# A convolution's first banded weight tile on GpSimd, held behind a row of sums of squares

## The chip, the cores and the metric

The kernel runs on one core of one Trainium2 chip. The metric is the device time of one execution in microseconds (us), smaller is better; the time given for a kernel is the median of several executions.

The engines of the core work side by side, each through its own instructions in order: TensorE does matrix products (PE in the profile, and PEld for its weight loads), VectorE (DVE), ScalarE (ACT) and GpSimd (POOL) work on tiles of 128 partitions, and SyncE (SP) issues most of the DMAs. An engine waits for another only where an instruction waits on a semaphore.

## The reference

One step of a streaming encoder with two layers, width 1024, in float32. It treats 512 frames of a new stream (the prompt) and 8 running streams of 16 frames (the sample group). Only the first layer matters here, and of it the part up to the convolution:

```python
def conv_module(h, hist, g, w_pw1, b_pw1, w_dw, b_dw, ln_g, ln_b, w_pw2, b_pw2):
    a, gate = jnp.split(rms_norm(h, g) @ w_pw1 + b_pw1, 2, axis=-1)
    glu = a * jax.nn.sigmoid(gate)
    full = jnp.concatenate([hist.astype(glu.dtype), glu], axis=1)
    y = lax.conv_general_dilated(full, w_dw[:, None, :], ...) + b_dw
    y = jax.nn.silu(layer_norm(y, ln_g, ln_b))
    return h + y @ w_pw2 + b_pw2, full[:, -CONV_HIST:]
```

`rms_norm` divides each frame by the root of its mean square over the 1024 features. The convolution is depthwise (each feature by itself), 31 taps wide and causal. After it come a layer norm over the features, a product with a 1024x1024 matrix, and a gated feed-forward block; the second layer is attention and a second feed-forward block, and a last norm.

## The kernel before, in words

The activations `h` lie with features on the partitions: 8 chunks of 128 features, 640 frames along the free dimension. The frames are worked in two groups: group 0 is frames 0 to 255 (the 128 sample frames and the first 128 of the prompt), group 1, the larger one, is frames 256 to 639.

**Products.** Every float32 weight tile is split into a rounded high part and the rest (`wsplit`): ScalarE writes the high part (`whi`, L156), VectorE and GpSimd write the rest (`wlo`, L160), each a share. In the first products `pool=2`, so the second half of a tile's 2048 columns is GpSimd's. Activations are split likewise by `xsplit` (L165 ScalarE, L166 VectorE). A product is three matmuls (L176 to L178).

**Root mean square.** `rms` calls `rstd_bc`: eight squares of the chunks (`square`, L185 on ScalarE, L188 on VectorE or GpSimd) are added up one after the other by `colmean` into `acc` (L201), TensorE sums over the partitions (L210), VectorE adds epsilon (L232), GpSimd raises to the power -0.5 (L236), and TensorE spreads the result over 128 partitions (L222). Then VectorE forms the eight normed chunks `n` (L249), and `xsplit` makes the products' operand `x`. For group 0 the adds are on VectorE; for group 1 the adds and five of the squares are on GpSimd.

**Gated product and convolution.** `glu(c, g)` makes feature chunk c of the gated product; VectorE writes it into `gs` (group 0, L392) or `gp` (group 1, L401), and for group 0 four copies on GpSimd (L396 to L399) put the prompt's overlapping frames in place. Each chunk's convolution is done in one of three ways: on VectorE (`conv`, L440 and L443, written into PSUM), on ScalarE and GpSimd (`conv_pool`, L422 and L423), or on TensorE (`conv_pe`, L475). The last one needs what `conv_pe_load` prepares: the weight tile `w4`, 32 banded 32x32 blocks that one GpSimd multiply (L450) makes from `i4`, four identity blocks, and `dwv`, the taps that a DMA from ScalarE's queue brings (L373), and `x4`, four shifted copies of the chunk that go by DMA through memory (`sc`, L458, and `x<-sc`, L461). Both tiles have one buffer, so a second `conv_pe` waits for the first.

**What sets the order.** The string `PLAN` lists the steps in the order in which they are written: `a0 y a1 a2 a4 x a3 a5 a6 l04 p04 ...` means glu of chunks 0, 1, 2 and 4 for group 0, then `x`, the root mean square of group 1, then more glu, then `l04`, the load for the TensorE convolution of chunk 4 in group 0, and `p04`, that convolution. Within this a list scheduler places every instruction as early as its inputs allow, by a priority that the code can raise (`tc.high_priority`). `tc.issue_after(ins)` is an edge for the scheduler: what is written inside it is placed after `ins`.

The multiply for `l04` has inputs that are there from the beginning (`i4`, `dwv`), so it is placed near the head of GpSimd's row, ahead of everything that group 0 asks of GpSimd. The multiply's tile is first read by `p04`.

Of the kernel before, what the change touches and what calls it, by code (L numbers as in the profile page):

```python
# [11 lines left out]
ALU = mybir.AluOpType  # L12
PSUM = bass.MemoryType.PSUM

P = 128
# [60 lines left out]
V_DW, V_DW4, V_NDW = 0, KT * W, KT * W + KT * 32  # L76
# [3 lines left out]
def tile_trunk(ctx, tc, xT, vecs, hist, w_pw1, w_pw2, w_in0, w_out0, w_in1, w_out1,  # L80
               w_kq, w_v, w_o, rel, kc, vc, nfin, y_out, convp_out, convs_out, k_out, v_out):
    nc = tc.nc
# [13 lines left out]
    def nm(s):  # L96
        uid[0] += 1
        return f"{s}_{uid[0]}"
# [79 lines left out]
            nc.tensor.matmul(ps, wh, xl, start=False, stop=(i == last))  # L178

    last = {}  # L180

    def square(s, n, eng="a"):
        q = tp.tile([P, 384], F32, tag="sq", name=nm("sq"))
        if eng == "a":
            nc.scalar.activation(out=q[:, :n], in_=s, func=AF.Square)  # L185
        else:
            e = nc.vector if eng == "v" else nc.gpsimd
            e.tensor_tensor(out=q[:, :n], in0=s, in1=s, op=ALU.mult)  # L188
        return q[:, :n]
# [155 lines left out]
    dwv = cp.tile([P, V_NDW], F32, name="dwv", tag="dwv")  # L345
# [14 lines left out]
    i4 = cst.tile([P, 32 + XPAD], F32, name="i4", tag="i4")[:, 0:32]  # L360
# [86 lines left out]

    def conv_pe_load(c, g):
        w4 = cp.tile([P, 32, 32], F32, tag="w4", name=nm("w4"))
        nc.gpsimd.tensor_tensor(  # L450
            out=w4, in0=i4[:, None, :].to_broadcast([P, 32, 32]),
            in1=dwv[:, V_DW4 + 32 * c:V_DW4 + 32 * c + 32].unsqueeze(2).to_broadcast([P, 32, 32]),
            op=ALU.mult)
        full = GSW if g == 0 else GPW
        wd = full - 4
        src = gsf if g == 0 else gp
        sc = dr.tile([P, GSW], F32, tag="sc", name=nm("sc"))
        nc.sync.dma_start(sc[:, 0:full], src[:, c, :])  # L458
        x4 = cp.tile([P, 4, GSW], F32, tag="x4", name=nm("x4"))
        for s in range(4):  # L460
            nc.sync.dma_start(x4[32 * s:32 * s + 32, :, 0:wd],  # L461
                              sc[:, s:s + wd].rearrange("(q p) w -> p q w", q=4))
        return w4, x4
# [60 lines left out]
    def step(op, arg):  # L524
# [6 lines left out]
        elif op == "b":  # L531
            pw1(g, 1)
        elif op == "y":
            load_x(1)
        elif op == "x":
            xs[1] = rms(1, V_NCONV, SSQ1, 8)
        elif op == "l":
            x4s[g, cs[0]] = conv_pe_load(cs[0], g)
        elif op == "p":
            conv_pe(cs[0], g, *x4s[g, cs[0]])  # L540
        elif op == "q":
            conv_pool(cs[0], g)
        elif op == "d":
            conv(cs, g)
        elif op == "s":
            if g == 0:
                nc.sync.dma_start(convs_out, gs[:, :, 0:8, :])
            else:
                nc.sync.dma_start(convp_out, gp[:, :, 384:384 + HIST])
        elif op == "n":  # L550
            zs[g] = conv_ln(g)
        elif op == "w":
            pw2(g, zs[g])
        elif op == "r":
            late[g] = (R0, R1)[g](g, V_NFFN)
        elif op == "f":
            ffn({0: hp0}, w_in0, w_out0, {0: late[0]}, (0,), (chunks.pop(0),), PFA)
# [354 lines left out]
    xps = ExitStack()  # L912
    xp = xps.enter_context(tc.tile_pool(name="xp", bufs=1, **tr))

    def after(ins):
        return tc.issue_after(ins.ins) if ins is not None else ExitStack()

    def tmp(t):
        return tp.tile([P, 384], F32, tag=t, name=nm(t))[:, 0:HT]

# [35 lines left out]
    def plain(j, jj, q, wts):  # L956
        wh, wl = wts
        c = TH[q]
        ps = []
        for ab in range(2):  # L960
            pt = bank()
            o = [(8 * ab + (k + 4 * ab) % 8) * P for k in range(KT)]
            with after(marks.get((j, q, ab))):
                mm3(pt[:, :HT], [(wh[:, i:i + P], wl[:, i:i + P]) for i in o],
                    [(raw_slot[k // 4][q][0][:, k % 4, :], raw_slot[k // 4][q][1][:, k % 4, :])
                     for k in range(KT)])
            ps.append(pt[:, :HT])
        with tc.high_priority(offset=HP):
            gate(ps[0], ps[1], hids[0], jj, c)
# [230 lines left out]
    for j in range(NPL, FT):  # L1200
        c, jj = where[j]
# [112 lines left out]
```

## Time and profile before

| what | us |
|---|---|
| median of 3 executions | 1543.46 |
| lowest and highest of them | 1538.12, 1545.01 |
| the profiled execution, its own time | 1541.31 |
| span of its trace | 1539.5 |
| busy in the span: PE, DVE, ACT, POOL | 1467.9, 1049.0, 667.1, 447.3 |
| instructions on POOL | 406 |

The profile comes from a single execution, by the hardware profiler. A row of its timeline has the start in us from the span's beginning, the length in us, engine, line of the code, operation, what is written and read with its shape, how many instructions were merged, and in square brackets how long the engine had been idle before and what ended that wait. Rows overlap a little at their ends. In a table of stretches, PEclk is the share of full TensorE speed that was granted. "PE mm" rows are matmuls, "mm" being the tile in PSUM.

### The profile page before, as it was taken

How to read it: one execution, taken by the hardware profiler on the slowest of the kernel's cores; microseconds unless marked ns; L12 is line 12 of the kernel's file. 1: busy time of each engine (PE TensorE's matmuls, PEld its weight loads, DVE VectorE, ACT ScalarE, POOL GpSimd, SP SyncE). 2: the span in 40 equal slices, each digit the busy share in tenths (PEclk: the TensorE clock that was granted, in tenths of full speed). 3: DMA queues.
4: the chain of work that ended last, by engine and by line, in shares of the span. 5: the costliest groups of instructions: out<-in, count | busy, mean ns of one | idle time of the engine just before them, and what ended most of it. 6: DMA issues, size and time to landing. Idle time of an engine off the chain costs nothing.

```text
span 1539.5 us, 27212 instructions
## 1 busy us (share of the span) xinstructions
PE 1467.9 (95%) x11054; PEld 1397.9 (91%) x11054; DVE 1049.0 (68%) x1890; ACT 667.1 (43%) x1196; POOL 447.3 (29%) x406
## 2 busy tenths in 40 slices
PE   5988898989999999999999999999999999999998
PEld 5878878988999999999988798896989999999998
DVE  6994999989555444556577767666796467467456
ACT  4544455545423323235455445343564144244144
POOL 6965458987401000001322111110421011011010
PEclk9989899999999999999999999999999999999999
DMA  7884334454421333432555545444103222222222
GB/s 261 249 219 143 123 103 162 146 183 151 151 83 56 123 123 123 126 120 96 196 184 195 170 151 199 150 158 151 32 25 117 76 83 89 76 83 90 76 83 83
DMA packets 57022, 200.54 MB, mean 130 GB/s; under 512 B 10176, under 2 KB 20672, under 8 KB 44096
## 3 DMA queue, kind: packets, MB, share of 16 engines
q1 hardware_dynamic: 56608, 198.48, 39.1%
q8 instruction: 87, 1.43, 0.4%
q10 hardware_dynamic: 288, 0.31, 0.1%
q14 instruction: 39, 0.32, 0.1%
HBM read 187.55 MB, written 11.22 MB: 129 GB/s over the span
## 4 chain that ended last, share of the span: by engine, by line
PE 73%; DVE 15%; issue 3%; ACT 3%; POOL 3%; DMA 3%; SPq 0%; POOLq 0%; ACTq 0%; DVEq 0%
PE mm L176 13%; PE mm L177 13%; PE mm L178 13%; PE pb L977 6%; DVE w L443 4%; PE pc L977 4%; DVE wlo L160 4%; PE pa L977 3%; PE w L803 1%; PE pb L176 1%; PE pb L178 1%; PE pb L177 1%; PE pa L178 1%; PE pa L176 1%; PE pa L177 1%
## 5 line engine op out<-in xcount | busy, mean ns | idle before, releaser
L177 PE MATMUL mm<-x,wlo 128*128 128x256 f32 (+1 forms) x1344 | 417.8, 313 | 15.8 <-DVE wlo L160 15.4
L176 PE MATMUL mm<-x,whi 128*128 128x256 f32 (+1 forms) x1344 | 414.4, 312 | 9.2 <-ACT x L165 6.9
L178 PE MATMUL mm<-x,whi 128*128 128x256 f32 (+1 forms) x1344 | 413.0, 311 | 2.5 <-DVE x L166 2.5
L177 PEld LDWEIGHTS mm<-x,wlo 128*128 128x128 f32 x1344 | 257.1, 191 | 19.4 <-DVE wlo L160 18.3
L176 PEld LDWEIGHTS mm<-x,whi 128*128 128x128 f32 x1344 | 255.1, 191 | 14.1 <-ACT x L165 7.7
L178 PEld LDWEIGHTS mm<-x,whi 128*128 128x128 f32 x1344 | 255.3, 191 | 5.2 <-DVE x L166 4.1
L156 ACT ACTIVATE whi<-raw 128x2048 fp32r<-128x2048 f32 (+2 forms) x87 | 143.9, 1658 | 171.9 <-PE mm L178 105.1
L160 DVE TENSOR_TENSOR wlo<-raw,whi 128x2048 fp32r<-128x2048 f32 (+5 forms) x87 | 156.4, 1801 | 44.7 <-ACT whi L156 44.0
L922 POOL TENSOR_TENSOR raw<-raw 128x512 f32<-128x512 f32 x38 | 56.4, 1485 | 326.4 <-DVE raw L922 255.2
L177 PE MATMUL mm<-hid,wlo 128*128 128x256 f32 (+1 forms) x352 | 107.6, 308 | 6.1 <-DVE wlo L160 6.1
L160 POOL TENSOR_TENSOR wlo<-raw,whi 128x1536 fp32r<-128x1536 f32 (+3 forms) x33 | 93.0, 2822 | 55.1 <-ACT whi L156 55.1
L178 PE MATMUL mm<-hid,whi 128*128 128x256 f32 (+1 forms) x352 | 105.8, 307 | 0.8 <-DVE hid L166 0.7
L443 DVE SCALAR_TENSOR_TENSOR w<-gp,dwv,w 128x384 f32<-128x384 f32 x180 | 104.4, 613 | 0.9
L176 PE MATMUL mm<-hid,whi 128*128 128x256 f32 (+1 forms) x352 | 104.4, 307 | 0.0
L201 POOL TENSOR_TENSOR acc<-sq,sq 128x384 f32<-128x384 f32 (+1 forms) x8 | 8.1, 1006 | 255.8 <-ACT sq L185 255.8
L156 ACT ACTIVATE whi<-rx 128x2048 fp32r<-128x2048 f32 (+1 forms) x30 | 54.0, 1800 | 54.0 <-PE mm L178 42.0
L177 PEld LDWEIGHTS mm<-hid,wlo 128*128 128x128 f32 x352 | 66.0, 188 | 7.1 <-DVE wlo L160 7.1
L160 DVE TENSOR_TENSOR wlo<-rx,whi 128x2048 fp32r<-128x2048 f32 (+4 forms) x30 | 62.9, 2098 | 13.3 <-ACT whi L156 12.4
L423 POOL TENSOR_TENSOR y<-y,cvt 128x256 f32<-128x256 f32 (+1 forms) x60 | 67.9, 1132 | 4.3 <-ACT cvt L422 2.2
L178 PEld LDWEIGHTS mm<-hid,whi 128*128 128x128 f32 x352 | 65.7, 188 | 1.2 <-DVE hid L166 1.2
L176 PEld LDWEIGHTS mm<-hid,whi 128*128 128x128 f32 x352 | 65.1, 188 | 0.3 <-ACT hid L165 0.3
L165 ACT ACTIVATE whi<-raw 128x1024 fp32r<-128x1024 f32 x38 | 39.4, 1054 | 54.2 <-DVE raw L922 19.1
(329 smaller groups left out, 3648.2 us busy)
## 6 DMA issues: line engine op xcount, KB each, us to landing
raw<-in_w_in SPq DMA_DIRECT2D x49, 1024.0 KB
raw<-in_w_out SPq DMA_DIRECT2D x28, 768.0 KB
cache<-in_ck SPq DMA_DIRECT2D x32, 512.0 KB
cache<-in_cv SPq DMA_DIRECT2D x32, 512.0 KB
raw<-in_w_pw SPq DMA_DIRECT2D x14, 1024.0 KB
rx<-in_w_in SPq DMA_DIRECT2D x13, 1024.0 KB
rx<-in_w_pw SPq DMA_DIRECT2D x8, 1024.0 KB
raw<-in_w_kq SPq DMA_DIRECT2D x8, 1024.0 KB
```

The costliest lines, as they stand in the source:

```text
L156: nc.scalar.activation(out=hi[:, a:b], in_=raw[:, a:b], func=AF.Copy)
L160: eng.tensor_tensor(out=lo[:, a:b], in0=raw[:, a:b], in1=hi[:, a:b].bitcast(F32), op=ALU.subtract)
L165: nc.scalar.activation(out=hi, in_=src, func=AF.Copy)
L176: nc.tensor.matmul(ps, wh, xh, start=(i == 0), stop=False)
L177: nc.tensor.matmul(ps, wl, xh, start=False, stop=False)
L178: nc.tensor.matmul(ps, wh, xl, start=False, stop=(i == last))
L201: last["acc"] = eng.tensor_tensor(out=acc[:, :n], in0=prev, in1=s(), op=ALU.add)
L423: nc.gpsimd.tensor_tensor(out=y[g][:, c, :], in0=y[g][:, c, :], in1=pr[:, :n], op=ALU.add)
L443: nc.vector.scalar_tensor_tensor(out=dst, in0=src, scalar=wj, in1=dst, op0=ALU.mult, op1=ALU.add)
L803: nc.tensor.matmul(st[32 * b:32 * b + 32, 0:512], qv[b], KC[b // 2][:, b % 2, :], start=True, stop=True)
L922: ENG[e].tensor_tensor(out=out, in0=a, in1=b, op=op)
L977: nc.tensor.matmul(ps, a[:, c], b[:, k, :], start=(first and k == 0 and i == 0), stop=(k == 3 and i == 2), skip_group_check=not first)
```

## The change

The helper `after`, which wraps the edge `tc.issue_after`, moves from the last part of the kernel to its head; that moves no instruction. `conv_pe_load` then uses it for chunk 4 of group 0, and for no other call: the multiply that makes `w4` is placed after `last["acc"]`, which at that point is the last add of the squares of group 1.

```diff
+    def after(ins):
+        return tc.issue_after(ins.ins) if ins is not None else ExitStack()
+
...
     def conv_pe_load(c, g):
         w4 = cp.tile([P, 32, 32], F32, tag="w4", name=nm("w4"))
-        nc.gpsimd.tensor_tensor(
-            out=w4, in0=i4[:, None, :].to_broadcast([P, 32, 32]),
-            in1=dwv[:, V_DW4 + 32 * c:V_DW4 + 32 * c + 32].unsqueeze(2).to_broadcast([P, 32, 32]),
-            op=ALU.mult)
+        with after(last["acc"] if (c, g) == (4, 0) else None):
+            nc.gpsimd.tensor_tensor(
+                out=w4, in0=i4[:, None, :].to_broadcast([P, 32, 32]),
+                in1=dwv[:, V_DW4 + 32 * c:V_DW4 + 32 * c + 32].unsqueeze(2).to_broadcast([P, 32, 32]),
+                op=ALU.mult)
```

The scheduler places the rest of the first layer anew around it. In the rows below the first number is the line (lines of the changed kernel are 3 or 4 higher), and the numbers in names tell buffers apart.

GpSimd at the head of the program, before. `w_92_736` is the tile w4 of chunk 4, `rst_15_155` the power of group 0, `sq` the squares of group 1.

```order
L363 TENSOR_TENSOR i_105<-i_105,ident 128x32 x2
L450 TENSOR_TENSOR w_92_736<-i_105,dwv 128x1024
L236 TENSOR_TENSOR rst_15_155<-rst_153,mhalf 128x2
L160 TENSOR_TENSOR wlo_195<-raw_193,whi_194 128x256 x4
L188 TENSOR_TENSOR sq_468<-h 128x384
```

The same place now:

```order
L366 TENSOR_TENSOR i_105<-i_105,ident 128x32 x2
L239 TENSOR_TENSOR rst_15_155<-rst_153,mhalf 128x2
L160 TENSOR_TENSOR wlo_195<-raw_193,whi_194 128x256 x4
L191 TENSOR_TENSOR sq_468<-h 128x384
L191 TENSOR_TENSOR sq_471<-h 128x384
```

The multiply has gone from here, and nothing has taken its place.

GpSimd where the squares of group 1 end, before. `acc_470` is their sum, `wlo_402` and `wlo_537` are GpSimd's halves of the weight tiles of chunks 4 and 3, `y_109` the convolution on GpSimd, `rst_61_497` the power of group 1.

```order
L201 TENSOR_TENSOR acc_470<-acc_470,sq_489 128x384
L396 COPY gs<-gs 128x7x16
...
L160 TENSOR_TENSOR wlo_402<-raw_400,whi_401 128x1024
L423 TENSOR_TENSOR y_109<-y_109,cvt_1226 128x256
...
L160 TENSOR_TENSOR wlo_537<-raw_535,whi_536 128x1024
L423 TENSOR_TENSOR y_109<-y_109,cvt_1229 128x256
L236 TENSOR_TENSOR rst_61_497<-rst_495,mhalf 128x3
```

And now:

```order
L204 TENSOR_TENSOR acc_470<-acc_470,sq_489 128x384
L454 TENSOR_TENSOR w_92_736<-i_105,dwv 128x1024
L399 COPY gs<-gs 128x7x16
...
L160 TENSOR_TENSOR wlo_402<-raw_400,whi_401 128x1024
L426 TENSOR_TENSOR y_109<-y_109,cvt_1226 128x256
...
L160 TENSOR_TENSOR wlo_537<-raw_535,whi_536 128x1024
L239 TENSOR_TENSOR rst_61_497<-rst_495,mhalf 128x3
L426 TENSOR_TENSOR y_109<-y_109,cvt_1229 128x256
```

The multiply stands behind the last add and ahead of four copies and both halves; the power of group 1 has gone ahead of one add of `y_109`.

VectorE from the epsilon of group 1 to its first normed chunk, before. `w_99` is the convolution on VectorE, `n_63_503` the first normed chunk.

```order
L232 TENSOR_SCALAR rst_495<-w_50_467 128x3
L440 TENSOR_SCALAR w_99_788<-gs,dwv,vec 128x256 x2
L443 SCALAR_TENSOR_TENSOR w_99_788<-gs,dwv,w_99_788 128x256 x3
L392 SCALAR_TENSOR_TENSOR gs<-t_48_458,t_49_460 128x16x16
L443 SCALAR_TENSOR_TENSOR w_99_788<-gs,dwv,w_99_788 128x256 x2
L160 TENSOR_TENSOR wlo_604<-rx_602,whi_603 128x1024
L443 SCALAR_TENSOR_TENSOR w_99_788<-gs,dwv,w_99_788 128x256 x3
L249 SCALAR_TENSOR_TENSOR n_63_503<-h,vec,w_50_467 128x384
```

And now:

```order
L235 TENSOR_SCALAR rst_495<-w_50_467 128x3
L443 TENSOR_SCALAR w_99_788<-gs,dwv,vec 128x256 x2
L446 SCALAR_TENSOR_TENSOR w_99_788<-gs,dwv,w_99_788 128x256 x5
L395 SCALAR_TENSOR_TENSOR gs<-t_48_458,t_49_460 128x16x16
L446 SCALAR_TENSOR_TENSOR w_99_788<-gs,dwv,w_99_788 128x256 x3
L160 TENSOR_TENSOR wlo_604<-rx_602,whi_603 128x1024
L446 SCALAR_TENSOR_TENSOR w_99_788<-gs,dwv,w_99_788 128x256
L252 SCALAR_TENSOR_TENSOR n_63_503<-h,vec,w_50_467 128x384
```

There are 9 steps of the convolution (lines L443, now L446) ahead of the first normed chunk where there were 8. From there to the last operand `x` of group 1 the order has 12 of them where it had 16, so 21 in all and not 24; the other instructions of that stretch are the same. On TensorE the products of chunk 3's first tile go ahead of those of chunk 4's second tile (`mm_543` ahead of `mm_433`), and the spreading of group 1's result (L222) goes six matmuls later, to the end of chunk 3's second tile. SyncE's row is the same as before.

More of the change, by code (lines that the diff above doesn't have):

```diff
@@ L913, in tile_trunk @@
     xp = xps.enter_context(tc.tile_pool(name="xp", bufs=1, **tr))
-    def after(ins):
-        return tc.issue_after(ins.ins) if ins is not None else ExitStack()
     def tmp(t):
```

## The prediction

> **What bounds the kernel now.** I read the page first, then a table of stretches, the chain of waits, and the timelines of single engines where the multiply stands and where it goes. The page's span and its slices (38.5 us each):
>
> ```profile
> span 1539.5 us, 27212 instructions
> PE   5988898989999999999999999999999999999998
> POOL 6965458987401000001322111110421011011010
> ```
>
> TensorE is full nearly everywhere; only the first ten slices have room. The table of stretches (busy us of each engine, then granted clock, DMA share, GB/s) says how much:
>
> ```profile
> 0.00:17.33 17.33, 2.21 (x8) 1.86 (x9) 10.53 (x23) 7.90 (x15) 7.04 (x21) 1.00 0.92 317
> 26.50:41.59 15.09, 13.69 (x114) 13.28 (x114) 6.29 (x5) 9.87 (x13) 15.09 (x18) 1.00 0.45 140
> 41.59:72.17 30.58, 30.58 (x294) 28.56 (x292) 29.89 (x43) 18.27 (x29) 26.84 (x37) 1.00 0.84 257
> 72.17:81.48 9.31, 5.12 (x23) 3.72 (x23) 9.31 (x13) 5.20 (x10) 8.26 (x7) 0.92 1.04 208
> 81.48:88.48 7.00, 7.00 (x25) 6.75 (x25) 7.00 (x14) 3.31 (x8) 5.57 (x8) 0.61 0.79 294
> 170.00:400.00 230.00, 209.09 (x1672) 200.64 (x1671) 215.97 (x320) 113.75 (x152) 172.00 (x87) 0.99 0.46 152
> ```
>
> The first 17.33 us have almost no TensorE work: the core waits for group 0's root mean square. From 41.59 to 72.17 TensorE is never idle. From 72.17 to 81.48 it is busy 5.12 of 9.31 us, while VectorE is busy all of it: TensorE waits there for the operand of group 1. So a microsecond on TensorE before 72.17 counts only if VectorE's chain to group 1's last chunk comes earlier too, because 4.19 us of idling stand behind it. The timeline has that end, and what follows it on TensorE, SyncE's transfers lying between:
>
> ```profile
> 80.38 1.05 DVE L166 TENSOR_TENSOR x<-n,x 128x384 fp32r<-128x384 f32 x1
> 81.48 0.69 PE L178 MATMUL mm<-x,whi 128*128 128x384 f32 x1 [0.79 <-DVE x L166]
> 88.48 3.66 PE L475 MATMUL mm<-x,w 128*32 128x256 f32 x64
> 93.52 9.64 DMA x<-sc
> 103.50 5.35 PE L475 MATMUL mm<-x,w 128*32 128x256 f32 x64 [2.84 <-DMA x<-sc]
> ```
>
> The last chunk (done at 81.43) starts the last products before the second TensorE convolution, whose end frees the one buffer of `x4`, which starts the 9.64 us transfer for which the third convolution waits 2.84 us. That string is rigid, so I take any shift of the last chunk as the shift of the end.
>
> **The change, part by part.** First, what leaves the head. The multiply, and VectorE and ScalarE beside it:
>
> ```profile
> 6.04 1.94 POOL L450 TENSOR_TENSOR w<-i,dwv 128x1024 f32<-128x1024 f32 x1 [3.35 <-DMA dwv<-in_vecs]
> 6.25 2.01 DVE L188 TENSOR_TENSOR sq<-h 128x256 f32<-128x256 f32 x1
> 8.19 1.40 DVE L201 TENSOR_TENSOR acc<-acc,sq 128x256 f32<-128x256 f32 x3
> 9.50 0.42 DVE L188 TENSOR_TENSOR sq<-h 128x256 f32<-128x256 f32 x1
> 8.63 0.42 ACT L185 ACTIVATE sq<-h 128x256 f32<-128x256 f32 x1 [1.97 <-DVE acc L201]
> 9.94 2.17 ACT L156 ACTIVATE whi<-raw 128x512 fp32r<-128x512 f32 x4
> 7.40 1.37 SPq L145 DMA_DIRECT2D raw<-in_w_pw  x3
> SPq L145 <- DMA h<-in_xa: 2.4, 2, 1.8
> ```
>
> The same square takes VectorE 2.01 us beside the multiply and 0.42 without it, and it ends 0.28 us after the multiply does (8.26 and 7.98). So the multiply costs the chain of group 0 up to 2.01 - 0.42 = 1.59 us. Not all of it comes back: ScalarE's third square (8.63) needs the second half of `h`, and SyncE's wait for that half ends at 7.40. The square can start there and no earlier, so 8.63 - 7.40 = 1.23 us are gained. I take 1.2, with 0 and 1.59 as ends. The low end is for the weights: ScalarE's high parts (9.94) follow its last square without a wait, so the trace does not show how much earlier their transfers would let them begin.
>
> The Trainium skill, in "SBUF — State Buffer", section "Who interferes with whom", says that a VectorE instruction with two SBUF inputs and a GpSimd instruction that reads SBUF exclude each other, whichever began first holding the port to its end. The trace agrees here (0.42 became 2.01), and the same rule speaks against the new place, where VectorE also has a two-input instruction ready.
>
> The new place, as GpSimd stands there before, with VectorE and ScalarE:
>
> ```profile
> 37.65 1.01 POOL L201 TENSOR_TENSOR acc<-acc,sq 128x384 f32<-128x384 f32 x1
> 39.31 2.40 POOL L160 TENSOR_TENSOR wlo<-raw,whi 128x1024 fp32r<-128x1024 f32 x1
> 43.76 0.25 POOL L397 COPY gs<-gs 128x84 f32<-128x84 f32 x1
> 47.30 1.06 POOL L236 TENSOR_TENSOR rst<-rst,mhalf 128x3 f32<-128x3 f32 x1
> 39.59 2.42 DVE L392 SCALAR_TENSOR_TENSOR gs<-t,t 128x256 f32<-128x256 f32 x1 [2.49 <-ACT t L386]
> 41.93 1.75 DVE L160 TENSOR_TENSOR wlo<-raw,whi 128x1024 fp32r<-128x1024 f32 x1
> 44.05 1.13 DVE L440 TENSOR_SCALAR w<-gs,dwv,vec 128x256 f32<-128x256 f32 x2 [0.30 <-POOL gs L397]
> 48.46 1.22 DVE L160 TENSOR_TENSOR wlo<-rx,whi 128x1024 fp32r<-128x1024 f32 x1
> 51.03 1.13 DVE L249 SCALAR_TENSOR_TENSOR n<-h,vec,w 128x384 f32<-128x384 f32 x2
> 86.12 4.39 DVE L443 SCALAR_TENSOR_TENSOR w<-gs,dwv,w 128x256 f32<-128x256 f32 x11
> ```
>
> GpSimd is full from 26.50 to 41.59 (15.09 of 15.09), so the multiply is not hidden on it. With the start 1.2 us earlier, the last add ends near 37.5 instead of 38.66, the multiply takes it to 39.4 (1.94, the price of its row), and everything queued behind it stands 1.94 - 1.2 = 0.7 us later than before. Queued are the copies of chunks 1 and 2, the halves of chunks 4 and 3, and the power of group 1, and behind those wait TensorE's second tiles and VectorE's convolution.
>
> VectorE's product `gs` at 39.59 already shows the price of this place: 2.42 us, ending 0.30 after GpSimd's 2.40 us half (41.71). Moved up by 1.2 it meets the multiply instead and ends near 39.7, 2.3 us earlier than before (42.01). It is no loss. Then VectorE's next two-input instruction, the half of `wlo` (41.93), meets GpSimd's half instead, which now runs from 40.1 to 42.5: it ends between 41.4 and 42.8, before 43.68 in any case. Its follower, the convolution's first step, waits for GpSimd's copies of chunk 2 (the second ends at 44.01 now). By the queue alone they come 0.7 late. I put the ends at 0, if the port no longer holds up the copies, and at 1.2, if VectorE's half goes ahead of GpSimd's (a half alone lasts 1.22, by the row at 48.46). So VectorE resumes 0 to 1.2 us late.
>
> The power of group 1 gains one add of `y` (0.7 us) and loses 0.7, so it stays near 48.4; TensorE spreads it six matmuls later, and `gs` of chunk 4 follows a tile that is later by one tile. By these, the first normed chunk (51.03) comes 0.1 to 1.5 us later; I take 0.8. From there to the last chunk, 12 convolution steps stand where 16 did, at 4.39 / 11 = 0.40 us: 4 x 0.40 = 1.6 us less. VectorE was busy all of that stretch, so they count in full. Sum for the last chunk: +0.8 - 1.6 = **-0.8 us**, between -1.5 and -0.1 by the bounds of the first term. The four steps that went behind it lie beside TensorE's products, not on the string.
>
> The head's 1.2 us are no further term: GpSimd's row eats them (0.7 late behind the multiply), and what is left is in the 0.1 to 1.5. That is the point of this forecast: the stall goes, and what is late next is GpSimd's queue at 40 us.
>
> Against the profiled execution's own 1541.31 (1.8 above its span) this gives 1540.5. That execution is 2.15 below the median of 1543.46, so in the measured median I expect 1543.46 - 0.8 = **1542.7 us**. The runs before lie from 1538.12 to 1545.01; about 0.5%, 7.7 us, is what a measurement of this kernel can tell from no change.
>
> **The rivals.**
>
> The gain stays whole. The head's 1.2 us pass through if GpSimd's halves are not what VectorE and TensorE wait for, and TensorE's idling at 72.17 to 81.48 shrinks so much that the clock stays up: 81.48 to 88.48 ran at 0.61, costing (1 - 0.61) x 7.0 = 2.7 us. Price: -1.2 - 1.6 - 2.7 = -5.5, so 1538.0. For it: VectorE's square did stall. Against it: GpSimd's full row. The Trainium skill, "TensorE: Matmul & The Clock Gate", section "What's actually happening", has a halved clock after an idle window of about 3.4 us, with windows that run free of the kernel; the row's 0.61 agrees in kind, and by that rule this cost may come or go between executions.
>
> It gets slower. The place is GpSimd behind the last add at 37.5 us. If GpSimd's half takes the port first at 40.1, VectorE's half ends at 42.8, TensorE, which now wants that half first, idles 1.8 us, and the copies come at the late bound: +1.5 on the first normed chunk. If the four steps saved are then spent waiting for ScalarE or for the port, the last chunk is 1.5 late, and one more stretch like that at 0.61 costs 2.7: +4.2, so 1547.7. It decides the sign when the first normed chunk comes later than 51.03 + 1.6 = 52.6. For it: GpSimd's row has no gap until far behind. Against it: TensorE's 4.19 us of idling absorb its own lateness.
>
> The square's stall has another cause than the multiply, so the change does not do its work: no gain in the head, GpSimd 1.94 late, first normed chunk about 1.2 later than I forecast, +0.4: 1543.9. Against it stands the end 0.28 us behind the multiply.
>
> The reordering further down decides. VectorE is busy 215.97 of the 230 us from 170 to 400, and TensorE waits there for its weights' rest:
>
> ```profile
> PE mm L177 <- DVE wlo L160: 9.0, 7, 2.6
> ```
>
> That is 9.0 us in seven waits between 170 and 260 us. The scheduler moved convolution steps and weights against each other there too; were all those waits lost or doubled, the time would be 1533.7 or 1551.7.
>
> **How the numbers follow.** Chances: the forecast 0.46, the whole gain 0.18, the slower case 0.18, no effect 0.08, the reordering 0.10. Beyond 7.7 us on the fast side are 0.04 of the whole gain (with more clock than one stretch) and 0.04 of the reordering: faster 0.08. On the slow side 0.04 of the slower case and 0.03 of the reordering: slower 0.07. Same: 0.85. The range goes from the whole gain (1538.0) to the slower case (1547.7), and on by about 2 and 1 us because the runs before spread further to the low side: 1536.0 to 1548.5.
>
> **What would show it right or wrong.** In the profile of the changed kernel: VectorE's square at 6.25 should last 0.42, and TensorE's first product should start near 16.1 instead of 17.33. GpSimd's multiply should stand near 37.5, with the half behind it starting near 40.1; the first normed chunk should be at 51 to 52.5 and the last chunk near 80.6. The distance from there to the second and third TensorE convolution should be as before. I am wrong if the square stays long, if the last chunk moves by more than 1.5 us either way, if TensorE's clock in the first 120 us is much changed, or if the time is made or lost behind 170 us.

## The result and the profile after

| | median, us | from | to | executions |
|---|---|---|---|---|
| before | 1541.88 | 1538.12 | 1545.01 | 6 |
| changed | 1554.63 | 1548.34 | 1560.25 | 6 |

The ratio is 1.0085, 95% interval 1.0066 to 1.0105: slower, by 12.7 us. The execution that was profiled, 1548.34 us, is the fastest of the six. Its span is 1546.6, 7.1 more than before; its trace therefore shows a little over half of the loss.

The head came out as forecast. VectorE's second square, GpSimd's multiply with the half behind it, and TensorE's first product, in the profile of the changed kernel:

```profile
6.33 0.42 DVE L191 TENSOR_TENSOR sq<-h 128x256 f32<-128x256 f32 x1
...
12.75 0.16 DVE L235 TENSOR_SCALAR rst<-w 128x2 f32<-128x2 f32 x1
...
37.64 1.91 POOL L454 TENSOR_TENSOR w<-i,dwv 128x1024 f32<-128x1024 f32 x1
...
40.41 3.43 POOL L160 TENSOR_TENSOR wlo<-raw,whi 128x1024 fp32r<-128x1024 f32 x1
16.20 0.58 PE L176 MATMUL mm<-x,whi 128*128 128x256 f32 x1 [1.02 <-ACT x L165]
```

VectorE from there to group 1's first normed chunk (`n`) and last operand chunk (`x`):

```profile
40.37 1.22 DVE L160 TENSOR_TENSOR wlo<-raw,whi 128x1024 fp32r<-128x1024 f32 x1 [0.54 <-ACT whi L156]
...
44.98 1.13 DVE L443 TENSOR_SCALAR w<-gs,dwv,vec 128x256 f32<-128x256 f32 x2 [3.32 <-POOL gs L400]
...
50.75 3.33 DVE L160 TENSOR_TENSOR wlo<-rx,whi 128x1024 fp32r<-128x1024 f32 x1
...
54.39 1.13 DVE L252 SCALAR_TENSOR_TENSOR n<-h,vec,w 128x384 f32<-128x384 f32 x2
...
77.85 0.92 DVE L166 TENSOR_TENSOR x<-n,x 128x384 fp32r<-128x384 f32 x1 [0.62 <-ACT x L165]
```

The first normed chunk is 3.4 us late (51.03 before), and the last operand chunk, ended at 78.77, is 2.7 us early (81.43). The second and third TensorE convolution, and SyncE's transfers between them, now; then SyncE's rows before:

```profile
84.63 3.66 PE L479 MATMUL mm<-x,w 128*32 128x256 f32 x64
...
103.88 5.91 PE L479 MATMUL mm<-x,w 128*32 128x256 f32 x64 [7.07 <-DMA x<-sc]
83.66 1.78 SPq L462 DMA_DIRECT2D sc<-gs  x2
...
91.66 1.76 SPq L465 DMA_DIRECT2D x<-sc  x4
```
```profile
83.28 1.78 SPq L458 DMA_DIRECT2D sc<-gs  x2
...
92.20 3.03 SPq L461 DMA_DIRECT2D x<-sc  x4
```

The second convolution is 3.9 us early, the third 0.4 late: TensorE waits 7.07 us for the transfers where it waited 2.84. So up to 105 us hardly anything is won or lost. The table of stretches, before and then changed (us, busy of PE, PEld, DVE, ACT and POOL, then the granted clock, the DMA share and GB/s), shows where the loss comes:

```profile
0.00:160.00 160.00, 128.67 (x983) 117.73 (x984) 121.94 (x204) 78.78 (x128) 104.83 (x124) 0.94 0.72 217
160.00:200.00 40.00, 37.85 (x308) 33.85 (x307) 39.34 (x57) 17.17 (x24) 21.60 (x12) 0.98 0.32 108
200.00:260.00 60.00, 52.91 (x407) 51.09 (x407) 59.96 (x106) 32.82 (x49) 41.97 (x22) 0.97 0.38 124
```
```profile
0.00:160.00 160.00, 125.81 (x978) 114.97 (x979) 116.39 (x202) 77.74 (x125) 105.32 (x124) 0.95 0.70 217
160.00:200.00 40.00, 37.07 (x298) 33.68 (x301) 38.66 (x56) 18.21 (x27) 18.22 (x12) 0.96 0.31 107
200.00:260.00 60.00, 51.91 (x382) 49.85 (x374) 59.89 (x93) 28.00 (x45) 37.11 (x19) 0.91 0.35 108
```

VectorE is busy all of 200 to 260 us in both, but gets through 93 instructions instead of 106. Nothing of the change lies there; the scheduler had put the rows in another order. TensorE's clock is lower there too, 0.91 for 0.97. It falls in short stretches in which about half of full speed is granted (0.51 from 241.5 to 248.0 us in the changed kernel); they are called half-clock stretches below. One place of it, VectorE and GpSimd, before and then changed:

```profile
210.68 0.42 DVE L166 TENSOR_TENSOR x<-n,x 128x256 fp32r<-128x256 f32 x1
...
211.53 0.56 DVE L401 SCALAR_TENSOR_TENSOR gp<-t,t 128x384 f32<-128x384 f32 x1
212.12 3.47 POOL L160 TENSOR_TENSOR wlo<-raw,whi 128x1536 fp32r<-128x1536 f32 x1 [14.01 <-ACT whi L156]
...
213.11 3.03 DVE L160 TENSOR_TENSOR wlo<-raw,whi 128x512 fp32r<-128x512 f32 x1
216.06 2.19 DVE L443 SCALAR_TENSOR_TENSOR w<-gp,dwv,w 128x384 f32<-128x384 f32 x4
```
```profile
214.04 3.46 POOL L160 TENSOR_TENSOR wlo<-raw,whi 128x1536 fp32r<-128x1536 f32 x1 [12.76 <-ACT whi L156]
214.38 3.54 DVE L404 SCALAR_TENSOR_TENSOR gp<-t,t 128x384 f32<-128x384 f32 x1
...
218.95 0.68 DVE L160 TENSOR_TENSOR wlo<-raw,whi 128x512 fp32r<-128x512 f32 x1
...
220.08 0.70 DVE L166 TENSOR_TENSOR x<-n,x 128x256 fp32r<-128x256 f32 x1
220.70 3.23 DVE L446 SCALAR_TENSOR_TENSOR w<-gp,dwv,w 128x384 f32<-128x384 f32 x6
```

Before, the product `gp` slips in ahead of GpSimd's share of `wlo` and lasts 0.56 us. Now it begins 0.34 us behind it and lasts 3.54, to 0.42 us past its end (217.50); and the last operand chunk `x`, which stood ahead of both, now stands behind them and ends at 220.78 instead of 211.10. From there the lateness grows to 9.1 us (group 1's `rst` of a later norm: 380.85 for 371.76) and is 7.1 at the end. This is what the experiments take apart.

### The profile page after: what moved, and what is told of

Its sections match the earlier page's. It is cut to its first block, busy times and chain, and to the rows that moved or that the text cites. A ratio compares the mean times of both kernels' runs of the same rounds, so it can differ in the third digit from the quotient of the medians.

```text
span 1546.6 us, 27210 instructions
## 1 busy us (share of the span) xinstructions
PE 1466.2 (95%) x11054; PEld 1396.4 (90%) x11054; DVE 1051.7 (68%) x1890; ACT 667.0 (43%) x1196; POOL 445.8 (29%) x406
## 4 chain that ended last, share of the span: by engine, by line
PE 71%; DVE 16%; issue 4%; POOL 3%; ACT 3%; DMA 2%; SPq 0%; POOLq 0%; DVEq 0%; ACTq 0%
PE mm L176 13%; PE mm L177 13%; PE mm L178 13%; PE pb L978 6%; DVE w L446 5%; DVE wlo L160 4%; PE pc L978 4%; PE pa L978 3%; PE w L807 1%; PE pb L176 1%; PE pb L177 1%; PE pb L178 1%; PE pa L178 1%; PE pa L176 1%; PE pa L177 1%
## 5 line engine op out<-in xcount | busy, mean ns | idle before, releaser
L446 DVE SCALAR_TENSOR_TENSOR w<-gp,dwv,w 128x384 f32<-128x384 f32 x180 | 104.0, 611 | 0.9
```

The costliest lines, as they stand in the source:

```text
L446: nc.vector.scalar_tensor_tensor(out=dst, in0=src, scalar=wj, in1=dst, op0=ALU.mult, op1=ALU.add)
```

## The experiments

In most of them the order of every engine is written down in the kernel as a table ("the rows"), so that one thing can be moved and nothing else follows. The edges that do it order a row and wait for nothing:

```diff
+by = {i.name: i for i in nc.cur_bb.bb.instructions}
+for row in ROWS:
+    for prev, name in zip(row, row[1:]):
+        tc.add_manual_dep(by[name], prev, NoSync, reason="row")
```

Short diffs show what was moved (the table makes the line numbers in the experiments' profiles some 90 higher); the ratio is always to the kernel before, measured on the same chip beside it.

**The place, or the other rows?** Four kernels, with three theories: A, the rows past 160 us make the loss; B, the multiply's new place makes it; C, the changed rows of the first 160 us make it. First, the rows of before with the multiply alone moved:

```diff
 GpSimd, rows of before
 L363 i_105<-i_105,ident
-L450 w_92_736<-i_105,dwv
...
 L201 acc_470<-acc_470,sq_489
+L450 w_92_736<-i_105,dwv
```

> Every engine's row of instructions is written down as in the kernel before; only the first w4 multiply stands behind the last add of the larger group's squares instead of at the head of GpSimd's row. Everything is computed. Theory A (the loss is made by the rest of the order, which came out differently past 160 us: the last x of the stage at 200 to 230 us behind VectorE's blocked gp copy): ratio to the kernel before 0.998 to 1.002, about 1541 us, first normed chunk later by 1 to 3 us, and no row past 160 us moved by more than 2 us. Theory B (the multiply's new place itself costs it): ratio 1.006 to 1.010, about 1554 us. Theory C (the changed rows of the first 160 us, through waits and the clock gate): 0.998 to 1.002, as A.

Measured: 1.0003 (0.9989 to 1.0016), 1540.6 us. In its trace the first normed chunk is 3.9 us late (54.97), where 1 to 3 were expected, and the last chunk 2.9 late (ended at 84.38); neither shows in the time. The reverse, the rows of the changed kernel with that one line back at the head:

> The rows of the changed kernel on every engine, written down, with the first w4 multiply put back to the head of GpSimd's row. Everything is computed. Theory A (late rows): ratio 1.006 to 1.011, about 1553 us, with the last x at 220 us again some 8 us late. Theory B (the multiply's place): 0.998 to 1.002. Theory C (early rows): 1.005 to 1.010.

Measured: 1.0081 (1.0061 to 1.0101), 1552.7 us: the whole loss, without the edge's own effect. B has fallen. Then the two halves of the rows, cut at about 160 us, where both orders have placed the same instructions:

```diff
-rows = changed
+rows = changed[:160 us] + before[160 us:]
```

> The rows of the changed kernel, the moved multiply among them, on every engine up to about 160 us, and those of the kernel before from there on. Everything is computed. Theory A (late rows): ratio 0.999 to 1.002, about 1543 us, the last x of the stage at 200 to 230 us late by no more than 2 us. Theory B (the multiply's place) and theory C (early rows): 1.006 to 1.010, about 1553 us.

```diff
-rows = changed
+rows = before[:160 us] + changed[160 us:]
```

> The rows of the kernel before, the multiply at GpSimd's head, on every engine up to about 160 us, and those of the changed kernel from there on. Everything is computed. Theory A (late rows): ratio 1.005 to 1.010, about 1553 us, the last x at 220 us some 7 to 10 us late. Theories B and C: 0.998 to 1.002, about 1542 us.

Measured: early rows 1.0013 (1.0000 to 1.0026), late rows 1.0052 (1.0032 to 1.0073), with the chunk at 220 us 5.9 us late in the trace, where 7 to 10 were expected. A holds and C has fallen; the two do not quite add up to the changed kernel's 1.0085, but the intervals allow it.

**One displaced chunk?** Theory A1 laid the late rows' loss on the chunk `x` shown above. Rows of before with only that chunk put late, and rows of the changed kernel with only that chunk put back:

```diff
 VectorE, rows of before
-L166 x_2036<-n_264_2065,x_2036
 L443 w_213_1631<-gp,dwv,w_213_1631
 L401 gp<-t_271_2159,t_272_2161
...
 L160 wlo_2230<-raw_2228,whi_2229
...
+L166 x_2036<-n_264_2065,x_2036
```

> Every row as in the kernel before, the first w4 multiply at GpSimd's head; only one operand chunk is put where the changed kernel has it: the last x of the f layer that starts at about 200 us (ScalarE's rounding of it behind the next t and whi, VectorE's low part of it behind the gp copy, one convolution step, wlo of the next stage and one more step). Everything is computed. Theory A1 (this one displaced chunk carries the loss of the late rows): the last x ends 5 to 9 us later than in the kernel before, the rows past 260 us 3 to 8 us later, ratio 1.002 to 1.005. Rival A2 (the whole re-interleaving of convolution steps, operand chunks and weights between 160 and 350 us): no row past 260 us later than 2 us, ratio 0.999 to 1.0015.

> Every row as in the changed kernel, the moved multiply among them; only that one operand chunk (ScalarE's rounding and VectorE's low part of the last x of the f layer at about 200 us) is put back ahead of the next t and of the gp copy. Everything is computed. Theory A1: the last x ends within 4 us of the kernel before, ratio to the kernel before 1.001 to 1.004, that is 0.4 to 0.7% below the changed kernel. Rival A2: 1.006 to 1.010, as the changed kernel.

Measured: 1.0020 (1.0008 to 1.0031), which is A1's number, and 1.0056 (1.0039 to 1.0074), which lies between A1's and A2's. The chunk is worth 0.2% where it is put late, and 0.3% where it is put back (1.0085 less 1.0056, from two sets of runs whose intervals overlap). That is a part, not the cause. (In the trace of the second kernel the chunk still ends 7.1 us later than before, where within 4 was expected; the profiled execution is the slowest of its six.) The trace of the kernel with the chunk put late shows its price: VectorE runs out of work until TensorE, late by the chunk, is done.

```profile
215.97 1.23 DVE L254 TENSOR_TENSOR x<-n,x 128x256 fp32r<-128x256 f32 x1
217.12 1.13 DVE L531 SCALAR_TENSOR_TENSOR w<-gp,dwv,w 128x384 f32<-128x384 f32 x2
221.36 0.42 DVE L382 TENSOR_TENSOR t<-t,mm 128x256 f32<-128x256 f32 x1 [3.10 <-PE mm L266]
```

**A better place.** Between its third square and the next add GpSimd idles about 2 us in the profile of before, waiting for ScalarE. The multiply fits there:

```diff
 GpSimd, rows of before
-L450 w_92_736<-i_105,dwv
...
 L188 sq_477<-h
+L450 w_92_736<-i_105,dwv
 L201 acc_470<-acc_470,sq_474
```

> Every row as in the kernel before; only the first w4 multiply stands behind GpSimd's third square of the larger group, where GpSimd waits some 2.0 us for ScalarE's square, instead of at the head of GpSimd's row. Everything is computed. All theories: VectorE's first square lasts 0.4 instead of 2.0 us, the first rst comes 1.2 us earlier, and the GpSimd work at 38 us is no later than in the kernel before. Theory A: what is gained at the head lasts, ratio 0.998 to 1.000. Rival (the half-clock stretches take the gain back or give more, as the waits fall): 0.999 to 1.002.

Measured: 1.0004 (0.9989 to 1.0019), in the rival's range and just outside that of A. Its trace has the gain (the rows at 430 us are 2.3 us earlier than before), its times do not tell it from nothing. The same place by a scheduling edge, with every row placed anew:

```diff
-with after(last["acc"] if (c, g) == (4, 0) else None):
+with after(last["p"][2] if (c, g) == (4, 0) else None):
```

> The same place for the multiply as in e7_gap (behind GpSimd's third square of the larger group), but by a scheduling edge as in the changed kernel, so that the rows of all engines come out anew; in them the last x of the f layer at about 200 us stands ahead of the gp copy. Everything is computed. Theory A1 (what counts is whether that chunk is displaced): the last x no more than 3 us later than in the kernel before, ratio 0.998 to 1.003. Rival A3 (any new order loses against the order before): 1.004 to 1.012.

Measured: 1.0095 (1.0077 to 1.0113), though the chunk is not displaced there (it ends 3.4 us later than before, where no more than 3 was expected). A1 has fallen and A3 held, for this order: the same move costs nothing in fixed rows and nearly 1% when the scheduler places the rest anew.

**What is it in the late rows?** Before the next runs the two traces were compared over the same twelve weight tiles: before from 169.4 to 258.2 us, changed from 171.2 to 267.3. The time went up by 96.1 - 88.8 = 7.3 us. VectorE's groups there (busy us, mean ns), before and then changed:

```profile
L443 DVE SCALAR_TENSOR_TENSOR w<-gp,dwv,w 128x384 f32<-128x384 f32 x85 | 49.8, 614 | 0.5
L160 DVE TENSOR_TENSOR wlo<-raw,whi 128x512 fp32r<-128x512 f32 (+3 forms) x8 | 16.1, 2014 | 0.0
L160 DVE TENSOR_TENSOR wlo<-rx,whi 128x512 fp32r<-128x512 f32 (+2 forms) x4 | 10.2, 2546 | 0.0
L166 DVE TENSOR_TENSOR hid<-t,hid 128x256 fp32r<-128x256 f32 x6 | 3.8, 626 | 0.0
L401 DVE SCALAR_TENSOR_TENSOR gp<-t,t 128x384 f32<-128x384 f32 x2 | 1.1, 552 | 0.0
```
```profile
L446 DVE SCALAR_TENSOR_TENSOR w<-gp,dwv,w 128x384 f32<-128x384 f32 x86 | 50.2, 612 | 0.6
L160 DVE TENSOR_TENSOR wlo<-raw,whi 128x512 fp32r<-128x512 f32 (+3 forms) x8 | 17.0, 2128 | 0.0
L160 DVE TENSOR_TENSOR wlo<-rx,whi 128x512 fp32r<-128x512 f32 (+2 forms) x4 | 11.1, 2783 | 0.0
L166 DVE TENSOR_TENSOR hid<-t,hid 128x256 fp32r<-128x256 f32 x6 | 5.2, 870 | 0.0
L404 DVE SCALAR_TENSOR_TENSOR gp<-t,t 128x384 f32<-128x384 f32 x2 | 4.1, 2047 | 0.0
```

The same instructions last longer: `wlo` 0.9 + 0.9, `hid` 1.4, `gp` 3.0, together 6.2 of the 7.3 us. All of these read two operands from SBUF. The lengthening lies inside their own time and no idle time stands ahead of it, so one engine can hold another without a semaphore; the sentence on waiting in the first section leaves this out. The convolution step `w`, whose sum lies in PSUM, lasts 0.61 in both, beside GpSimd or not (604 to 624 ns over all 180 of them before). The Trainium skill, "SBUF — State Buffer", section "Who interferes with whom", draws the line at the same place: two SBUF inputs contend with a GpSimd instruction that reads SBUF, one does not.

So theory P: in this stretch, where VectorE is the busiest engine, the orders differ by how long GpSimd's shares hold VectorE. Rival W: by operands that come later and by TensorE's waits and clock. Two kernels put convolution steps ahead of VectorE's share of `wlo` wherever GpSimd's share would hold it, on the rows of before and on those of the changed kernel; for instance

```diff
 VectorE, rows of before, GpSimd's share of wlo_2230 running
+L443 four convolution steps
 L160 wlo_2230<-raw_2228,whi_2229
-L443 four convolution steps
```

> Every row as in the kernel before, the multiply at GpSimd's head, but VectorE's: between 150 and 325 us, where VectorE's half of a wlo lasts longer than 1.2 us because GpSimd's half of the same wlo is running, the next one to five convolution steps (43 steps at fifteen places, as many as fit before GpSimd's half ends in the profile of before) are put ahead of VectorE's half. Everything is computed. Theory P (VectorE is the bound there, and time goes where its two-input instructions are held by GpSimd's): up to 43 x 0.52 = 22 us of VectorE's time come free, TensorE takes up a part, ratio 0.990 to 0.998. Rival W (the order costs by what TensorE waits for and by half-clock stretches, not by how long VectorE's halves last): 0.999 to 1.005, since the weights' low parts come no earlier.

> The same rule on the rows of the changed kernel (48 steps at fourteen places put ahead of VectorE's halves between 150 and 335 us, by the changed kernel's own profile). Everything is computed. Theory P: the changed kernel's disadvantage goes, ratio to the kernel before 0.993 to 1.002. Rival W: 1.006 to 1.011, as the changed kernel.

Measured: 0.9995 (0.9982 to 1.0009) and 1.0037 (1.0023 to 1.0052). The first is W's number, though the rows at 430 us are 3.5 us earlier than before in its trace, which is of its fastest execution. The second lies between both: half of the loss went, and half stayed. Two more took GpSimd's share away in that stretch, on both sets of rows. They leave out the low part of the columns that are GpSimd's, half to three quarters of each of the thirteen weights (not a quarter, as the expectation has it):

```diff
-eng.tensor_tensor(out=lo[:, a:b], in0=raw[:, a:b],
-                  in1=hi[:, a:b].bitcast(F32), op=ALU.subtract)
+eng.memset(lo[:, a:b].bitcast(F32), 0.0)
```

> Every row as in the kernel before; the thirteen GpSimd halves of wlo from 169 to 262 us are replaced by a fill with zeros, which reads nothing, so that the lower-order part of a quarter of those weights' columns is left out. Theory P: VectorE's halves there last 0.6 to 0.7 us and the rows at 262 us come 8 to 16 us earlier than in the kernel before, ratio 0.990 to 0.997. Rival W: 0.997 to 1.001. The number that tells is the difference to e12_after_no_half.

> Every row as in the changed kernel, with the same thirteen GpSimd halves replaced by a fill with zeros and the same part of the weights left out. Theory P (what differs between the two orders in this stretch is how long VectorE is held): its ratio stands no more than 0.004 above that of e11_before_no_half. Rival W (the order itself, by operands and weights that come later): it stands 0.007 to 0.010 above it, as the changed kernel above the one before.

Measured: 0.9922 (0.9906 to 0.9937) and 0.9948 (0.9933 to 0.9962). The distance of the two orders is 0.0026 instead of 0.0085: P's number, not W's. So some 70% of what tells the orders apart hangs on GpSimd's shares in this stretch (by the intervals, roughly 45 to 95%). But a fill does two things: it does not hold VectorE, and it is done earlier, as it does not wait for the high part. TensorE's waits between 160 and 350 us, in the order before, changed, changed rows with steps ahead, and both with the fill (in all, times, longest), fall with the fill:

```profile
PE mm L177 <- DVE wlo L160: 17.3, 15, 2.6
```
```profile
PE mm L177 <- DVE wlo L160: 21.9, 14, 3.7
```
```profile
PE mm L264 <- DVE wlo L247: 19.0, 14, 3.6
```
```profile
PE mm L271 <- DVE wlo L254: 11.3, 11, 1.9
```
```profile
PE mm L271 <- DVE wlo L254: 11.6, 11, 2.4
```

With the shares the changed rows make TensorE wait 4.6 us longer; with the fill 0.3. Theory Q therefore: the shares cost by ending late, and the holding is only beside it. The last four tell, by the rule of the steps applied once more to each set (and the multiply in GpSimd's gap on the rows of before), and by another division of the thirteen tiles:

```diff
-c = b - (b - a) * pool // 4
+c = b - (b - a) * (min(pool, 2) if 14 <= halves[0] <= 26 else pool) // 4
```

> The rows of e9_late_halves with the rule applied once more by its own profile (24 more steps at eleven places ahead of VectorE's halves), and the first w4 multiply in GpSimd's idle gap as in e7_gap. Everything is computed. If time goes by how long VectorE is held (theory P): 0.994 to 0.998. If by when GpSimd's halves themselves end (theory Q: TensorE waits for them, and VectorE's holding is only beside it): 0.998 to 1.001, as e7_gap and e9_late_halves.

> The rows of e10_after_late_halves with the rule applied once more by its own profile (17 more steps at six places). Everything is computed. Theory P: a further part of the 0.37% that was left goes, ratio to the kernel before 0.999 to 1.003. Theory Q: 1.003 to 1.006, as e10_after_late_halves.

> Every row as in the kernel before, but in the thirteen weights from 169 to 262 us GpSimd computes half of wlo and VectorE half, where GpSimd had three quarters of most of them. Everything is computed. VectorE's own work grows by about 0.53 us for each of some ten weights (its half of 1024 columns lasts 1.22 in the profile of before where it is not held, that of 512 columns 0.69), and GpSimd's halves shorten from 3.5 to 2.4 us. Theory Q: the weights' low parts come about 1 us earlier each, ratio 0.994 to 0.998. Theory P: holding shrinks by 1.1 and VectorE's work grows by 0.5 for each, ratio 0.996 to 0.999. Rival (VectorE's greater part decides): 1.001 to 1.005.

> Every row as in the changed kernel, with the same division of the thirteen weights. Everything is computed. Theories P and Q: the distance to e15_before_half is smaller than the 0.0085 between changed kernel and kernel before, 0.003 to 0.006, as GpSimd's halves that make it are a third shorter. Rival (the order itself): 0.007 to 0.010.

Measured: 0.9964 (0.9951 to 0.9977), 1.0039 (1.0024 to 1.0054), 0.9982 (0.9967 to 0.9997) and 1.0057 (1.0034 to 1.0079). On the rows of before P's number comes, for the second round of steps and the multiply in the gap together, which were not measured apart: this version is faster than both kernels by more than the interval, its rows at 430 us are 6.6 us earlier than before, and TensorE's waits are down to

```profile
PE mm L264 <- DVE wlo L247: 15.4, 16, 2.1
```

On the changed rows nothing more is won, as Q has it. The shorter shares on the rows of before give 0.9982, in P's range and at the edge of Q's; they leave the orders 0.0075 apart, which is the rival's number against both. No one theory has all four.

The traces tell more than these ratios. The last table gives, for one execution of each kernel, when VectorE began its share of the first of the twelve tiles and of the tile behind the twelfth:

| | first tile, us | tile behind the twelfth, us | between |
|---|---|---|---|
| before | 169.44 | 258.25 | 88.8 |
| changed | 171.26 | 267.36 | 96.1 |
| before, steps ahead | 170.87 | 254.72 | 83.9 |
| changed, steps ahead | 173.62 | 261.85 | 88.2 |
| before, fill | 168.48 | 246.09 | 77.6 |
| changed, fill | 171.52 | 248.71 | 77.2 |
| before, steps twice, multiply in the gap | 169.40 | 252.66 | 83.3 |
| changed, steps twice | 175.69 | 264.55 | 88.9 |
| before, shorter shares | 169.92 | 257.07 | 87.2 |
| changed, shorter shares | 172.75 | 265.95 | 93.2 |

With the fill both orders need the same time, so in these executions the shares make the whole difference of this stretch; whether by holding VectorE or by ending late, the runs do not separate. The steps ahead shorten it in both orders, and the changed rows then need no more than the rows of before did. With the shorter shares 6.0 us of difference stay, and `gp` is still held on the changed rows: it begins at 215.29, behind GpSimd's share, and lasts 2.48 us instead of 0.55. What is left of the changed rows' loss with the steps ahead, some 0.4%, lies outside the stretch in these executions: the two kernels with steps come into it 4.2 and 6.3 us later than before (with the fill the two orders are 3.0 apart there). 0.1% of it may be the early rows; for the rest the runs do not separate the steps put ahead between 150 and 170 us, transfers that come later, and half-clock stretches.

## Why the prediction was wrong

**What held.** The square's stall was the multiply's (0.42 instead of 2.01), the gain in group 0 was 1.2 us (`rst` at 12.75, before 13.96), and TensorE began at 16.20 for a forecast 16.1. The multiply stood at 37.64 for 37.5, GpSimd's share behind it at 40.41 for 40.1. The place by itself cost nothing that can be measured (1.0003), as forecast.

**"The first normed chunk comes 0.1 to 1.5 us later."** It came 3.4 later. The term counted GpSimd's queue and one share of `wlo`. It left out that the next share on VectorE (1.22 at 48.46 before) would meet GpSimd's: 3.33 at 50.75, beside GpSimd's 2.35 from 50.64:

```profile
50.64 2.35 POOL L160 TENSOR_TENSOR wlo<-rx,whi 128x1024 fp32r<-128x1024 f32 x1
```

It also fails as a point of decision: it was later than the 52.6 at which the slower case was to begin, and yet the last chunk came 2.7 early (0.8 early was forecast). The four convolution steps fewer are only 2.0 us of that (8.7 to 6.7). The greater part is a term that the sum does not have: the eight operand chunks `x`, which read two operands from SBUF, last 5.2 us together instead of 10.3. From the first normed to the last operand chunk, before and then changed:

```profile
L166 DVE TENSOR_TENSOR x<-n,x 128x384 fp32r<-128x384 f32 x8 | 10.3, 1284 | 0.0
```
```profile
L166 DVE TENSOR_TENSOR x<-n,x 128x384 fp32r<-128x384 f32 x8 | 5.2, 679 | 0.6 <-ACT x L165 0.6
```

Before, the longest of them (2.75 from 56.40) ended 0.42 us behind a share of GpSimd's (3.38 from 55.35). The new order met fewer of these; nothing in the forecast foresaw that.

**"That string is rigid."** It was not. The second convolution passed on more than the gain (3.9 for 2.7), as TensorE ran the stretch ahead of it at a clock of 1.00 instead of 0.61, a piece of the rival in which the gain stays whole. The third passed on none: the transfers for it were issued only 0.5 us earlier (91.66 for 92.20) and lasted longer (10.54 us for 9.64). They were not issued earlier because they also wait for the store of chunk 7 (`sc`, 83.66 for 83.28), which VectorE's and GpSimd's work feeds. SyncE's waits ahead of them, before and then changed:

```profile
SPq L461 <- DMA sc<-gs: 4.0, 1, 4.0
SPq L461 <- PE mm L475: 1.5, 1, 1.5
```
```profile
SPq L465 <- DMA sc<-gs: 4.8, 1, 4.8
```

Before, TensorE's buffer came last, by 1.5 us; now it is free early and the store comes last. The gain therefore ended at 103.88 us, and the forecast of -0.8 had no way to the end. The first experiment says the same from the other side: its last chunk is 2.9 us late, and its time is that of before.

**"The reordering further down decides", chance 0.10.** This is what happened, and it went beyond the slow price that was put on it (1551.7; the median is 1554.63). The step of the prediction that failed is here: in the sum of -0.8 the rows past 160 us stand at nothing, without a reason, and the chance that they count is put at 0.10. The first experiments show the opposite: the edge is worth nothing (1.0003), the order that came with it 0.8% (1.0081), and the rows past 160 us alone 0.5% (1.0052). Another edge with a harmless place brought an order that lost 0.95%. Two new orders out of two lost, which is no law; both lie in a stretch where TensorE has 9.0 us of waits for one kind of tile and VectorE no idle time. Two signs that the prediction had set against itself came true: the last chunk moved by more than 1.5 us, and the time was lost behind 170 us.

**The range.** Its upper end, 1548.5, would have held the profiled execution, by luck, as that is the fastest of six, and not the median. The executions of the changed kernel follow TensorE's clock: 1548.34 us at a granted mean of 0.989, 1552.39 and 1552.82 at 0.986, 1556.45 at 0.984, 1558.63 at 0.983, 1560.25 at 0.982. The profile of before, at 0.988, stood where most of its runs stand (0.986 to 0.991 in those beside the first four experiments, median 0.989). The changed kernel's median clock is 0.985. By its own spread, 11.9 us for 0.007, the 0.004 between the two medians are 6.8 us, an estimate: about half of the 12.7. The forecast had half-clock stretches as single events of 2.7 us in the first 120 us, not as a level that another order can shift. Another order need not shift it: the kernel with the chunk put back lost 0.56% at a median clock of 0.9885.

## What to carry to other kernels

A scheduling edge is two changes, the one that is meant and a new order of everything behind it; write down the old order, move the one instruction, and measure the two apart before judging the edge. Where VectorE has no idle time, count its two-input instructions that will lie beside GpSimd's shares, and fill those stretches with work that reads one operand from SBUF (here 0.9964 at best, with the multiply in GpSimd's gap and on one order; a first round alone gave 0.9995, and on the other order half of the loss stayed). Before calling a chain rigid, list everything that its DMA waits for, not only what came last.

## What the runs showed of the hardware

- A VectorE instruction with two SBUF inputs that starts behind a GpSimd share waits for its end and then takes about its own time: 1.22 became 3.33 (50.75 to 54.08, GpSimd's share ending at 52.99). GpSimd is held likewise: its share of 2.40 us lasted 3.43 when VectorE's 1.22 us began 0.04 us ahead of it.
- A convolution step with one operand in PSUM is not lengthened: mean 614 and 612 ns over 85 and 86 of them in a stretch full of GpSimd's shares, and none of the 180 before lasts more than 624.
- A fill of GpSimd's does not lengthen VectorE's share: in the changed rows with the fill, a 128x512 share that began at 227.56, inside a fill from 226.85 to 228.24, lasted 0.69 us; beside a share of GpSimd's such a one lasted up to 3.30.
- The run-to-run spread of this kernel goes with TensorE's clock: 1.7 us of time for each 0.001 of granted mean, where 0.001 of 1550 us is 1.55 us. The Trainium skill, "TensorE: Matmul & The Clock Gate", section "What's actually happening", has a free-running window of about 3.4 us; by that rule the same waits cost more or less from one execution to the next. The traces agree: in the clock records all half-clock stretches, but for the one at the very end, last one to four times 3.41 us. Before, they begin at 80.1, 103.9, 151.7, 216.6 and 271.2 us (then twice more), each a whole number of such windows behind the last; in the changed kernel they begin at 53.9, 101.7, 152.9, 221.1, 241.6 and 279.2, on a grid of the same step with another start.
